# Sums over channels for four kinds of norm: products of split squares with a 0/1 matrix, in place of token-major sums spread back by an identity

## The chip, the cores and the metric

The kernel runs on one core of a Trainium2 chip. The time is that of one execution on the device in microseconds, measured over several runs; a profile is one further execution, read from the hardware profiler's records.

## The reference

The reference is one inference step of a layer with three branches between two half-step SwiGLU FFNs. It takes 512 prompt tokens and 8 x 8 sample tokens, so N = 576 tokens of 1024 channels; all in float32. The places where the change works are the norms, cut out here:

```python
def _rmsnorm(x, g):
    return x * lax.rsqrt(jnp.mean(x * x, axis=-1, keepdims=True) + 1e-6) * g

x = x + 0.5 * _swiglu(_rmsnorm(x, ffn1_norm), ffn1_w_up, ffn1_w_down)
h = _rmsnorm(x, mix_norm)
# RWKV-7 branch: 8 heads of 64 channels
kk = hd(k * k_k)
kk = kk / jnp.maximum(jnp.sqrt(jnp.sum(kk * kk, axis=-1, keepdims=True)), 1e-12)
...  # the recurrence over the tokens gives o
mean = jnp.mean(o, axis=-1, keepdims=True)
var = jnp.mean(jnp.square(o - mean), axis=-1, keepdims=True)
o = (o - mean) * lax.rsqrt(var + 64e-5) * gn_g + gn_b
# convolution branch: 256 channels
cm = jnp.mean(c, axis=-1, keepdims=True)
cv = jnp.mean(jnp.square(c - cm), axis=-1, keepdims=True)
c = (c - cm) * lax.rsqrt(cv + 1e-5) * conv_ln_g + conv_ln_b
...  # cross-attention branch, gated merge
x = x + 0.5 * _swiglu(_rmsnorm(x, ffn2_norm), ffn2_w_up, ffn2_w_down)
y = _rmsnorm(x, final_norm)
```

## The kernel before

**Layout.** Activations are channel-major: 128 channels in the partitions, 576 tokens along the free axis, worked on in two halves of 288. A projection (`mm3k`, L91) is made with float32 accuracy out of three float32r products: weights and activations are each split in two parts (`split`, L76 to L78: a cast by ScalarE to the high part, a subtraction by VectorE to the low part), and high x high, high x low, low x high are added in PSUM. The parts of the weights live in the ring `wq` with three slots each for `wh` and `wl` (`wload`, L64).

**Norms.** A sum over channels runs across partitions. `sums` (L111) takes 128 tokens of the squares as the stationary operand and a column of ones (or two columns, one for each head) as the moving one, in float32: its result is token-major, tokens in the partitions. Square root and reciprocal are then small (3, 5 or 10 columns). `spread` (L122) brings the values back to every channel by a float32 product with the identity, after `heads` (L133) has widened them for the two heads of a tile. Five places use this: the start of both FFNs (`rstd`, `rows`, L263 to L277), the norms that follow the FFNs (half by half, L337 to L370), the convolution's layer norm (L517 to L523), the norm of `kk` in `prep` (L685 to L694), and the group norm in `chain` (L752 to L765).

**Stages.** First comes FFN 1 (until about 425 us), then the three branches, then the merge and FFN 2. The branches follow a list of steps, `PLAN` (L24): P, I, J and B are prep, inverse, joined blocks and chain of one of four pairs of heads; A is the attention, G and C the convolution, X, Y and Z are fillers, projections of the gates and branches (`gate`, `gated`, L625 to L640), nearly all L91. A chain (B) runs eight chunks of 64 tokens one after another (`chunks`, L851): each needs the state of the one before, and goes from products to copies and back four times. Then come the sample chunk, and the group norm.

**Order.** Each engine issues in an order that is fixed when the kernel is built. The framework interleaves the steps of `PLAN` on each engine as far as dependences and buffers let it; a slot of a ring is given in the order of the program, so an instruction that needs a slot stays behind the earlier holders of that slot. TensorE, VectorE and ScalarE then each work through their own list in order; an instruction that waits for another engine holds those behind it.

Of the kernel before, what the change touches and what calls it, by code (L numbers as in the profile page):

```python
# [14 lines left out]
D = 1024  # L15
# [14 lines left out]
# columns of the packed parameter vectors  # L30
# [7 lines left out]
# columns of the packed constants  # L38
# [8 lines left out]
class _Builder:  # L47
# [16 lines left out]
    def wload(self, src, n, pool=None, tag="", cap=512):  # L64
        """A weight tile as two float32r parts whose sum is the float32 weight: f(part, from, to)."""
# [17 lines left out]
    def mm3(self, p, w, x, n, h, m=128):  # L83
        """p = w^T x for half h of the tokens, with float32 accuracy: hi*hi + hi*lo + lo*hi."""
        c = slice(h * H, (h + 1) * H)
        for k in range(n):
            self.mm3k(p, w(0, k * m, (k + 1) * m), w(1, k * m, (k + 1) * m), x[k], c, k, n)
# [5 lines left out]
    def proj(self, src, x, n=8, m=128):  # L93
        """The two halves of w^T x in PSUM."""
        w = self.wload(src, n * m)
        ps = []
        for h in range(2):
            p = self.bank()[:m, :H]
            self.mm3(p, w, x, n, h, m)
            ps.append((slice(h * H, (h + 1) * H), p))  # L100
        return ps

    def full(self, tag, *ops):
        """The two halves of the sum of float32 products lhs [K, 128]^T rhs [K, N] in PSUM."""
# [7 lines left out]
    def sums(self, tag, ops, sel, c):  # L112
        """Sums over channels, as sel [128, w] selects them, for the tokens of c: [128 tokens, block * w] in PSUM."""
# [7 lines left out]

    def spread(self, tag, r, c=slice(0, N)):  # L122
        """Token-major values r [128 tokens, block, 128 channels], 512 tokens at a time, channel-major in PSUM."""
# [9 lines left out]
    def heads(self, t, r):  # L133
        """[128 tokens, (block, head)] as [128 tokens, block, 128 channels], in t"""
        t = t.rearrange("p (b c) -> p b c", c=64)
        self.A.copy(t, r.unsqueeze(2).broadcast_to([128, 10, 64]))
        return t.rearrange("p (b h) c -> p b (h c)", h=2)

    @staticmethod
    def blocks(c):  # L140
        """Blocks of 128 tokens that cover c, as (first token, rows at the start that the block before holds)."""
# [7 lines left out]
    def build(self):  # L149
        tc, a = self.tc, self.a  # L150
        with ExitStack() as st:
# [9 lines left out]
            self.eps = cp.tile([128, 2], F32, name="eps")  # L161
# [9 lines left out]
            with ExitStack() as sf:  # L171
# [16 lines left out]
                self.dma(self.cst, a["cst"])  # L188
                self.G.memset(self.eps[:, 0:1], 64e-5)
                self.G.memset(self.eps[:, 1:2], 1e-5)  # L190
                self.A.activation(self.eps[:, 0:1], self.eps[:, 0:1], AF.Copy)
# [60 lines left out]
    @staticmethod  # L252
    def padded(t):
        """The chunks of 64 + 1 columns and the sample blocks of 8 + 1"""
        return _q8(t[:, :520], 65), _q8(t[:, 520:592], 9)
# [7 lines left out]
    def rstd(self, fp, ss, h):  # L263
        """1/sqrt(mean square + 1e-6) of the tokens of half h, token-major."""
# [6 lines left out]

    def rows(self, fp, t, h):
        """The values t of the tokens of half h in every partition."""
# [13 lines left out]
    def ffn(self, x, hp, fp, g, wu, wd, done, raw=None, mid=None, kv=()):  # L287
        """x += FFN(norm(x)) / 2, the last block of it half by half of the tokens, each handed to done.
        raw: the weights of the first three projections, by 128 input channels, which run as the channels come in."""
# [19 lines left out]
        r = [self.rstd(fp, ss, h) for h in range(2)]  # L309
        r = [self.rows(fp, t, h) for h, t in enumerate(r)]  # L310
# [32 lines left out]
        for i in range(2):  # L343
            s = slice(i * H, (i + 1) * H)
            for m in range(8):
# [4 lines left out]
                if i == 1 and m == 1:  # L350
                    r = self.rstd(fp, ss, 0)
                if i == 1 and m == 3:
                    done(x, fp, slice(0, H), self.rows(fp, r, 0))
# [16 lines left out]
    def mem_k(self):  # L370
        """Memory keys of the prompt, channel-major."""
# [10 lines left out]
    def mem_v(self):  # L382
        """Memory values of the prompt, token-major."""
# [13 lines left out]
    def mem_keep(self, kv):  # L397
        """Keys block-diagonal for a pair of heads, and values."""
# [18 lines left out]
    def shifted(self, m, out, zp):  # L417
        """out = z + (previous z - z) * mu for the m-th 128 channels of the shifted projection."""
# [77 lines left out]
    def conv(self, ap, us):  # L496
# [20 lines left out]
        p = self.sums("g", sq, self.con("ones", 1), slice(0, N))  # L517
        r = ap.tile([128, 5], F32, name="rt")
        A.activation(r, p, AF.Sqrt, scale=1.0 / 256, bias=self.eps[:, 1:2])
        V.reciprocal(r, r)  # L520
        for c, p in self.spread("g", r.unsqueeze(2).broadcast_to([128, 5, 128])):
            for j in range(2):
                V.tensor_tensor(cs[j][:, c], cs[j][:, c], p, ALU.mult)  # L523
# [10 lines left out]
    def softmax(self, ap, p, s):  # L534
        """exp(p / 8 - max) over the last axis of p [128, n, 256] into s; returns the reciprocals of its sums."""
# [11 lines left out]
    def attention(self, ap, op):  # L547
# [8 lines left out]
        # prompt  # L556
# [26 lines left out]
        # samples: the rows of a request are its (head, token) pairs  # L583
# [47 lines left out]
    def gated(self, pool, n, wname, y, i, first):  # L631
        """Adds sigmoid(gate n) * (y @ w) to the merged branches in DRAM (first: writes it)."""
# [10 lines left out]
    def prep(self, j):  # L643
# [6 lines left out]
        def parts(t, o=0):  # L650
            """prompt [128, 8, 64 of q] and sample [128, 8, 8 of q] views of a dense tile"""
# [3 lines left out]
        # decay and its running products within a chunk; a zero column restarts the product  # L655
        sg = b1.tile([128, 640], F32, name="u1", bufs=2)[:, :N]
# [28 lines left out]
        sq = b1.tile([128, 640], F32, name="u1", bufs=2)[:, :N]  # L685
        A.activation(sq, k, AF.Square, scale=par("kk", j))
        p = self.sums("g", [sq], bd[:, ::64], slice(0, N))
        rt = b1.tile([128, 10], F32, name="rt")
        A.activation(rt, p, AF.Sqrt)
        V.tensor_scalar(rt, rt, 1e-12, None, ALU.max)  # L690
        V.reciprocal(rt, rt)
        nr = b1.tile([128, 640], F32, name="u1", bufs=2)[:, :N]
        for c, p in self.spread("g", self.heads(b1.tile([128, 640], F32, name="u1", bufs=2), rt)):
            V.scalar_tensor_tensor(nr[:, c], k[:, c], par("kk", j), p, ALU.mult, ALU.mult)  # L694
# [20 lines left out]
        # products of the rows within a chunk: rows (k, b) by source token, columns (r, a) by token  # L715
# [13 lines left out]
    def chain(self, j):  # L729
# [5 lines left out]
        # token-major keys and values  # L735
# [15 lines left out]
        # group norm, bonus and gate  # L751
        sq, rs = (b3.tile([128, 640], F32, name="u2", bufs=2)[:, :N] for _ in range(2))  # L752
# [6 lines left out]
        p = self.sums("c", [sq], con("bd")[:, ::64], slice(0, N))  # L759
        rt = b3.tile([128, 10], F32, name="rt")  # L760
        A.activation(rt, p, AF.Sqrt, scale=1.0 / 64, bias=self.eps[:, 0:1])
# [309 lines left out]
```

## Time and profile before

| | us |
|---|---|
| median of 3 runs | 1533.83 |
| lowest and highest run | 1531.67, 1535.93 |
| span of the profiled execution | 1531.9 |
| busy: VectorE / ScalarE | 818.2 / 583.4 |
| first sums of FFN 1 / of FFN 1's end | 27.13 / 418.93 |
| recurrence of the last chain, four chunks | 967.1 to 984.2 |

The span of the profiled execution runs from its first to its last instruction. In the rows of the profile, PE is TensorE's products, PEld its loading of stationary operands, DVE is VectorE, ACT is ScalarE; L91 is line 91 of the kernel. A float32 product appears as two records, a float32r product as one.

### The profile page before, as it was taken

Reading aid. Unit: us, or ns where it says so; the run is one execution under the profiler, and the core shown is the slowest. Engines: PE = TensorE matmul, PEld = TensorE weight load, DVE = VectorE, ACT = ScalarE, POOL = GpSimd, SP = SyncE. Lnnn points to the kernel's source line nnn. Section 1 sums busy time; section 2 is a strip of 40 time slices with the busy share of each in tenths; the row PEclk is TensorE's granted clock in tenths of the full one; section 3 lists DMA queues with packets and bytes.
Section 4 is the critical chain, followed back from the end, with each engine's and each line's share of the span. In section 5 each row is a group of like instructions: output and inputs, shape, how many; then the busy total and the mean of one; then the engine's idle time right before and its main releaser. Section 6 shows DMA issues by size and latency. Waiting matters only on the chain.

```text
span 1531.9 us, 26990 instructions
## 1 busy us (share of the span) xinstructions
PE 1505.6 (98%) x11194; PEld 1430.4 (93%) x11194; DVE 818.2 (53%) x1639; ACT 583.4 (38%) x1155; POOL 4.5 (0%) x21
## 2 busy tenths in 40 slices
PE   8999999999999999999999999999999999999997
PEld 8999999999998889878879879889999999999997
DVE  6443344334584559768466455376444434443454
ACT  6232223223457645445346533343332222222331
POOL 0000000000000000000000000000000000000000
PEclk9999999999999999999899999999999999999998
DMA  5222222222533143123223124274212222222231
GB/s 189 83 83 83 84 83 83 83 83 83 163 106 131 38 153 75 58 77 106 63 64 94 52 73 119 67 246 160 84 69 83 83 83 84 83 83 83 84 110 63
DMA packets 90711, 144.64 MB, mean 94 GB/s; under 512 B 43148, under 2 KB 52748, under 8 KB 90588
## 3 DMA queue, kind: packets, MB, share of 16 engines
q1 hardware_dynamic: 90012, 142.33, 28.8%
q8 instruction: 87, 1.43, 0.4%
q10 hardware_dynamic: 576, 0.59, 0.1%
q14 instruction: 36, 0.29, 0.1%
HBM read 126.36 MB, written 16.53 MB: 93 GB/s over the span
## 4 chain that ended last, share of the span: by engine, by line
PE 93%; DVE 3%; ACT 2%; DMA 1%; issue 1%; SPq 0%; DVEq 0%; ACTq 0%
PE p L91 79%; PE g L724 1%; PE c L842 1%; PE c L846 1%; PE c L839 1%; PE g L109 1%; DVE pr L801 1%; PE c L109 1%; PE c L874 1%; PE c L872 1%; DVE tt L803 1%; PE c L857 1%; PE c L894 0%; PE p L129 0%; PE g L129 0%
## 5 line engine op out<-in xcount | busy, mean ns | idle before, releaser
L91 PE MATMUL p<-xh,wl 128*128 128x288 f32 (+1 forms) x2080 | 620.9, 299 | 1.5 <-DVE wl L78 1.5
L91 PE MATMUL p<-xl,wh 128*128 128x288 f32 (+1 forms) x2080 | 621.9, 299 | 0.0
L91 PE MATMUL p<-xh,wh 128*128 128x288 f32 (+1 forms) x2080 | 620.9, 299 | 0.9 <-ACT r L276 0.6
L77 ACT CAST wh<-w 128x512 fp32r<-128x512 f32 (+1 forms) x371 | 226.1, 611 | 558.0 <-PE p L91 540.2
L91 PEld LDWEIGHTS p<-xh,wh 128*128 128x128 f32 (+1 forms) x2080 | 391.6, 188 | 8.0 <-issue 3.1
L91 PEld LDWEIGHTS p<-xh,wl 128*128 128x128 f32 (+1 forms) x2080 | 391.4, 188 | 7.2 <-issue 3.3
L91 PEld LDWEIGHTS p<-xl,wh 128*128 128x128 f32 (+1 forms) x2080 | 391.7, 188 | 6.5 <-issue 4.4
L78 DVE TENSOR_TENSOR wl<-w,wh 128x512 fp32r<-128x512 f32 (+1 forms) x371 | 251.5, 679 | 265.4 <-ACT wh L77 252.7
L91 PE MATMUL p<-hl,wh 128*128 128x288 f32 x512 | 151.0, 295 | 0.0
L91 PE MATMUL p<-hh,wh 128*128 128x288 f32 x512 | 151.0, 295 | 0.0
L91 PE MATMUL p<-hh,wl 128*128 128x288 f32 x512 | 150.7, 294 | 0.0
L91 PEld LDWEIGHTS p<-hh,wl 128*128 128x128 f32 x512 | 96.1, 188 | 0.0
L91 PEld LDWEIGHTS p<-hl,wh 128*128 128x128 f32 x512 | 96.1, 188 | 0.0
L91 PEld LDWEIGHTS p<-hh,wh 128*128 128x128 f32 x512 | 96.0, 188 | 0.0
L326 DVE TENSOR_TENSOR t<-p,r 128x288 f32<-128x288 f32 x88 | 40.2, 457 | 90.6 <-PE p L91 90.6
L337 DVE SCALAR_TENSOR_TENSOR x<-p,x 128x288 f32<-128x288 f32 x64 | 29.3, 458 | 68.9 <-PE p L91 68.9
L77 ACT CAST hh<-t 128x576 fp32r<-128x576 f32 (+1 forms) x50 | 30.8, 616 | 77.5 <-DVE t L331 57.5
L91 PE MATMUL p<-hh,whd 128*128 128x288 f32 x192 | 56.9, 296 | 0.0
L91 PE MATMUL p<-hl,whd 128*128 128x288 f32 x192 | 56.5, 294 | 0.0
L91 PE MATMUL p<-hh,wld 128*128 128x288 f32 x192 | 56.5, 294 | 0.0
L320 DVE TENSOR_TENSOR t<-p,r 128x288 f32<-128x288 f32 x88 | 39.9, 455 | 24.4 <-PE p L91 21.3
L78 DVE TENSOR_TENSOR hl<-t,hh 128x576 fp32r<-128x576 f32 (+1 forms) x50 | 34.3, 686 | 33.2 <-ACT hh L77 33.2
(312 smaller groups left out, 1887.0 us busy)
## 6 DMA issues: line engine op xcount, KB each, us to landing
w<-wu SPq DMA_DIRECT2D x85, 512.0 KB
w<-win SPq DMA_DIRECT2D x44, 512.0 KB
w<-wd SPq DMA_DIRECT2D x32, 512.0 KB
w<-wd SPq DMA_DIRECT2D x16, 384.0 KB
d_mb<-gate SPq DMA_DIRECT2D x16, 288.0 KB
w<-wo SPq DMA_DIRECT2D x8, 512.0 KB
x<-x SPq DMA_DIRECT2D x8, 288.0 KB
d_x<-x SPq DMA_DIRECT2D x16, 144.0 KB
```

The lines of the kernel that those rows point to most:

```text
L77: self.A.copy(hi, x)
L78: self.V.tensor_tensor(lo, x, hi.bitcast(F32), ALU.subtract)
L91: self.T.matmul(p, l, x[r][:, c], start=k == 0 and i == 0, stop=k == n - 1 and i == 2)
L109: self.T.matmul(p, l, r[:, c], start=i == 0, stop=i == len(ops) - 1)
L320: V.tensor_tensor(t1[:, c], q, ri, ALU.mult)
L326: V.tensor_tensor(t2[:, c], q, ri, ALU.mult)
L337: V.scalar_tensor_tensor(x[m][:, c], p, 0.5, x[m][:, c], ALU.mult, ALU.add)
L724: T.matmul(ps[:, i * 128:(i + 1) * 128], kb[o, c + i].rearrange("p a t -> p (a t)"), ra[o, c + i].rearrange("p a t -> p (a t)"), start=Tru ...
L801: V.tensor_tensor(pr, tt[:, :n, :e].unsqueeze(2).broadcast_to([np_, n, m, e]), l3[:, t:e, :e].unsqueeze(1).broadcast_to([np_, n, m, e]), A ...
L803: V.tensor_reduce(tt[:, :n, t:e], pr, op=ALU.add, axis=AX.X)
L839: T.matmul(ps[64:, 64 * h:64 * h + 64], gr[:64, h, c, 64:], vu[:64, c, 64 * h:64 * h + 64], start=h == 0 or not inter, stop=not inter)
L842: T.matmul(ps[64:, :128], l, r, start=False, stop=i == len(inter) - 1)
```

## The change

`sums` stays for one use; `heads` is gone. The new `totals` splits the squares as weights and activations are split, into slots of the same ring `wq`, and multiplies both parts by a 128 x 128 matrix of zeros and ones as the stationary operand, 288 tokens at a time. The products are float32r, and their result is channel-major already: each channel holds the sum of its group. Square root and reciprocal then run over 288 or 576 columns in 128 partitions instead of 3, 5 or 10 columns. At the end of an FFN only the first half of the tokens goes this way; the second half keeps `rstd` and `rows`. Two copies of the 0/1 matrices are cast once at the start. The lines of the changed kernel lie some 12 further on (L869 is L857 of before, L884 L872, L886 L874, L854 L842, L851 L839, L858 L846, L769 L756), and comments were taken out.

```diff
+    def totals(self, tag, t, sel, c=slice(0, N)):
+        for o in range(c.start, c.stop, H):
+            hl = [self.wq.tile([128, 512], F32R, name="w" + i)[:, :H] for i in "hl"]
+            self.split(hl[0], hl[1], t[:, o:o + H])
+            p = self.bank(tag)[:, :H]
+            for i, t_ in enumerate(hl):
+                self.T.matmul(p, sel, t_, start=i == 0, stop=i == 1)
+            yield slice(o, o + H), p
...
+            self.sel = {t: cp.tile([128, 128], F32R, name="sel" + t) for t in ("ones", "bd")}
...
+    def rfull(self, fp, ss, h):
+        r = fp.tile([128, H], F32, name="r" + str(h), bufs=1)
+        for _, p in self.totals("p", ss, self.sel["ones"], slice(h * H, (h + 1) * H)):
+            self.A.activation(r, p, AF.Sqrt, scale=1.0 / D, bias=self.eps[:, 2:3])
+        self.V.reciprocal(r, r)
+        return r
...
-        r = [self.rstd(fp, ss, h) for h in range(2)]
-        r = [self.rows(fp, t, h) for h, t in enumerate(r)]
+        r = [self.rfull(fp, ss, h) for h in range(2)]
...
                 if i == 1 and m == 1:
-                    r = self.rstd(fp, ss, 0)
+                    r = self.rfull(fp, ss, 0)
                 if i == 1 and m == 3:
-                    done(x, fp, slice(0, H), self.rows(fp, r, 0))
+                    done(x, fp, slice(0, H), r)
...
-        p = self.sums("g", sq, self.con("ones", 1), slice(0, N))
-        r = ap.tile([128, 5], F32, name="rt")
-        A.activation(r, p, AF.Sqrt, scale=1.0 / 256, bias=self.eps[:, 1:2])
+        V.tensor_tensor(sq[1], sq[0], sq[1], ALU.add)
+        r = ap.tile([128, N], F32, name="sg", bufs=2)
+        for c, p in self.totals("g", sq[1], self.sel["ones"]):
+            A.activation(r[:, c], p, AF.Sqrt, scale=1.0 / 256, bias=self.eps[:, 1:2])
         V.reciprocal(r, r)
-        for c, p in self.spread("g", r.unsqueeze(2).broadcast_to([128, 5, 128])):
-            for j in range(2):
-                V.tensor_tensor(cs[j][:, c], cs[j][:, c], p, ALU.mult)
+        for j in range(2):
+            V.tensor_tensor(cs[j], cs[j], r, ALU.mult)
...
-        p = self.sums("g", [sq], bd[:, ::64], slice(0, N))
-        rt = b1.tile([128, 10], F32, name="rt")
-        A.activation(rt, p, AF.Sqrt)
-        V.tensor_scalar(rt, rt, 1e-12, None, ALU.max)
-        V.reciprocal(rt, rt)
-        nr = b1.tile([128, 640], F32, name="u1", bufs=2)[:, :N]
-        for c, p in self.spread("g", self.heads(b1.tile([128, 640], F32, name="u1", bufs=2), rt)):
-            V.scalar_tensor_tensor(nr[:, c], k[:, c], par("kk", j), p, ALU.mult, ALU.mult)
+        nr = b1.tile([128, N], F32, name="u1", bufs=2)
+        for c, p in self.totals("g", sq, self.sel["bd"]):
+            A.activation(nr[:, c], p, AF.Sqrt)
+        V.tensor_scalar(nr, nr, 1e-12, None, ALU.max)
+        V.reciprocal(nr, nr)
+        V.scalar_tensor_tensor(nr, k, par("kk", j), nr, ALU.mult, ALU.mult)
...
-        p = self.sums("c", [sq], con("bd")[:, ::64], slice(0, N))
-        rt = b3.tile([128, 10], F32, name="rt")
-        A.activation(rt, p, AF.Sqrt, scale=1.0 / 64, bias=self.eps[:, 0:1])
+        rt = b3.tile([128, N], F32, name="u2", bufs=2)
+        for c, p in self.totals("c", sq, self.sel["bd"]):
+            A.activation(rt[:, c], p, AF.Sqrt, scale=1.0 / 64, bias=self.eps[:, 0:1])
         V.reciprocal(rt, rt)
-        for c, p in self.spread("c", self.heads(b3.tile([128, 640], F32, name="u2", bufs=2), rt)):
-            V.tensor_tensor(rs[:, c], rs[:, c], p, ALU.mult)
+        V.tensor_tensor(rs, rs, rt, ALU.mult)
```

The change also moves instructions that it does not name. The first place is TensorE in one chunk of the last chain. This is the list of before, from the product with the state that gives the outputs (c<-ra,st) to the one that gives the next state (c<-vu,kbt); the rows p<- are projections of a filler, with xh and xl the two parts of the activations.

```order
L874 MATMUL c<-ra,st_4891 128x64
L842 MATMUL c<-st_4892,ra 64x128
L91 MATMUL p<-xh_4502,wl 128x288
L91 MATMUL p<-xh_4488,wh 128x288
L91 MATMUL p<-xl_4489,wh 128x288
L839 MATMUL c<-vu,gr 64x64 x2
L91 MATMUL p<-xh_4488,wl 128x288
L846 MATMUL c<-xs,gr 64x64 x2
L91 MATMUL p<-xh_4490,wh 128x288
L91 MATMUL p<-xl_4491,wh 128x288
L91 MATMUL p<-xh_4490,wl 128x288
L857 MATMUL c<-vu,kbt 128x128
```

This is the same piece of the list of the changed kernel:

```order
L886 MATMUL c<-ra,st_4885 128x64
L854 MATMUL c<-st_4883,ra 64x128
L851 MATMUL c<-vu,gr 64x64 x2
L858 MATMUL c<-xs,gr 64x64 x2
L869 MATMUL c<-vu,kbt 128x128
L884 MATMUL c<-gr,vu 64x64 x2
```

The projections are gone from between the chunk's products; in the four chains, 30 chunk updates stand like this, and only two intervals between updates (one each in the second and third chain) hold projections, 96 and 66 of them, in a row.

The second place is TensorE at the group norm of the first chain, before: c<-ra,cst are the products that subtract the mean, c<-cst,u the sums.

```order
L756 MATMUL c<-ra,cst 128x320
L756 MATMUL c<-ra,cst 128x256
L91 MATMUL p<-xl_4493,wh 128x288
L91 MATMUL p<-xh_4492,wl 128x288
L91 MATMUL p<-xh_4494,wh 128x288
L91 MATMUL p<-xl_4495,wh 128x288
L91 MATMUL p<-xh_4494,wl 128x288
L119 MATMUL c<-cst,u_7041 128x2 x2
L91 MATMUL p<-xh_4496,wh 128x288
L91 MATMUL p<-xl_4497,wh 128x288
```

And after, with c<-wh,selbd and c<-wl,selbd the new products of the split squares, and c<-lg,wg those of the branch's output gate:

```order
L769 MATMUL c<-ra,cst 128x320
L769 MATMUL c<-ra,cst 128x256
L129 MATMUL c<-wh,selbd 128x288 x2
L109 MATMUL c<-lg_4879,wg_4870 128x288
L129 MATMUL c<-wl,selbd 128x288
L109 MATMUL c<-aux,wg_4871 128x288
L129 MATMUL c<-wl,selbd 128x288
L91 MATMUL p<-xh_4481,wh 128x288
L91 MATMUL p<-xl_4482,wh 128x288
```

The five projections between the centering and the first sums are gone; the new products follow the centering at once, and the projections come behind them.

More of the change, by code (lines that the diff above doesn't have):

```diff
@@ L131, in spread @@
             yield d, p
[L133 to L137, printed above, removed]
     @staticmethod
@@ L160, in build @@
             self.cst = cp.tile([128, _NCC], F32, name="cst")
-            self.eps = cp.tile([128, 2], F32, name="eps")
+            self.eps = cp.tile([128, 3], F32, name="eps")
+            self.sel = {t: cp.tile([128, 128], F32R, name="sel" + t) for t in ("ones", "bd")}
             self.omu = cp.tile([128, 15], F32, name="omu")
@@ L188, in build @@
                 self.dma(self.cst, a["cst"])
+                for t, s in self.sel.items():
+                    self.A.copy(s, self.con(t))
                 self.G.memset(self.eps[:, 0:1], 64e-5)
                 self.G.memset(self.eps[:, 1:2], 1e-5)
+                self.G.memset(self.eps[:, 2:3], 1e-6)
                 self.A.activation(self.eps[:, 0:1], self.eps[:, 0:1], AF.Copy)
@@ L654, in prep @@
         k, r, v = tmp("k"), tmp("r"), b2.tile([128, N], F32, name="v")
-        sg = b1.tile([128, 640], F32, name="u1", bufs=2)[:, :N]
+        sg = b1.tile([128, N], F32, name="u1", bufs=2)
         for c, p in self.full("g", (self.wda[:64, 128 * j:128 * j + 128], self.la[:64])):
@@ L684, in prep @@
         self.shifted(4 + j, k, b1)
-        sq = b1.tile([128, 640], F32, name="u1", bufs=2)[:, :N]
+        sq = b1.tile([128, N], F32, name="u1", bufs=2)
         A.activation(sq, k, AF.Square, scale=par("kk", j))
-        p = self.sums("g", [sq], bd[:, ::64], slice(0, N))
-        rt = b1.tile([128, 10], F32, name="rt")
-        A.activation(rt, p, AF.Sqrt)
-        V.tensor_scalar(rt, rt, 1e-12, None, ALU.max)
-        V.reciprocal(rt, rt)
-        nr = b1.tile([128, 640], F32, name="u1", bufs=2)[:, :N]
-        for c, p in self.spread("g", self.heads(b1.tile([128, 640], F32, name="u1", bufs=2), rt)):
-            V.scalar_tensor_tensor(nr[:, c], k[:, c], par("kk", j), p, ALU.mult, ALU.mult)
+        nr = b1.tile([128, N], F32, name="u1", bufs=2)
[4 more added lines that the diff above has]
+        V.scalar_tensor_tensor(nr, k, par("kk", j), nr, ALU.mult, ALU.mult)
         for o, x, y in zip(ra_a, parts(nr), before):
@@ L749, in chain @@
         self.sample_chunk(j, gr, kbt, vu, ra, gc)
-        sq, rs = (b3.tile([128, 640], F32, name="u2", bufs=2)[:, :N] for _ in range(2))
+        sq, rs = (b3.tile([128, N], F32, name="u2", bufs=2) for _ in range(2))
         for c0, c1 in ((0, 5), (5, 9)):
@@ L899, in sample_chunk @@
             s = slice(64 * h, 64 * h + 64)
-            vx = b3.tile([128, 640], F32, name="u2", bufs=2)[:, :NB * 64].rearrange("p (b v) -> p b v", v=64)
+            vx = b3.tile([128, N], F32, name="u2", bufs=2)[:, :NB * 64].rearrange("p (b v) -> p b v", v=64)
             V.tensor_tensor(vx, vu[:, 8:9, s].broadcast_to([128, NB, 64]),
```

## The prediction

> **What bounds the kernel now.** The first views are the page's busy times, the shares of the chain of waits, and the clock row of the slices.
>
> ```profile
> span 1531.9 us, 26990 instructions
> PE 1505.6 (98%) x11194; PEld 1430.4 (93%) x11194; DVE 818.2 (53%) x1639; ACT 583.4 (38%) x1155; POOL 4.5 (0%) x21
> PE 93%; DVE 3%; ACT 2%; DMA 1%; issue 1%; SPq 0%; DVEq 0%; ACTq 0%
> PEclk9999999999999999999899999999999999999998
> ```
>
> TensorE is busy for 98% of the span, 93% of the chain that ended last is its work, and it runs almost always at full clock. So two things move the time: work that leaves TensorE, and any place where it has to wait that it did not have before. The second view cuts the span into stretches. After the span come busy time and count of PE, PEld, DVE, ACT and POOL, then the granted clock, the DMA share and GB/s.
>
> ```profile
> 30.00:420.00 390.00, 390.00 (x2932) 389.81 (x2933) 177.94 (x310) 113.18 (x182) 0.00 (x0) 1.00 0.27 89
> ...
> 737.30:740.70 3.40, 3.40 (x74) 3.15 (x73) 1.65 (x6) 0.83 (x3) 0.00 (x0) 1.00 0.17 55
> 740.70:744.10 3.40, 3.40 (x21) 3.34 (x19) 1.01 (x2) 0.58 (x1) 0.00 (x0) 0.51 0.02 5
> ...
> 945.60:949.00 3.40, 1.36 (x36) 1.25 (x37) 0.00 (x0) 1.31 (x5) 0.00 (x0) 0.99 0.94 279
> 949.00:952.40 3.40, 3.40 (x41) 3.19 (x39) 0.42 (x1) 1.43 (x4) 0.00 (x0) 0.50 0.20 66
> ```
>
> The first row is the first FFN: 390.00/2932 = 0.133 us for each product of 128x288 (nearly all are L91's). The others show what happens where L91 is missing. A stretch of 3.4 us whose 74 products are small ones is followed by one at clock 0.51, though PE counts as busy throughout. A stretch with PE busy for only 1.36 us is followed by 0.50. The third view is L91 alone in two stretches (busy PE, busy PEld, clock).
>
> ```profile
> 737.30:740.70 3.40, 0.00 (x0) 0.00 (x0) 1.00 0.17 55
> ...
> 967.10:984.20 17.10, 10.85 (x53) 7.52 (x53) 1.00 0.22 74
> ```
>
> The first of them had no L91. The second is four chunks of the last chain, with 53 L91, 13 for each chunk, and a clock of 1.00. **The chains are covered by the fillers' projections now.** The last view is the timeline of one chunk there:
>
> ```profile
> 977.51 0.34 PE L872 MATMUL c<-gr,vu 128*64 128x64 f32 x4
> 977.78 0.43 PE L874 MATMUL c<-ra,st 128*128 128x64 f32 x2
> 978.14 0.43 PE L842 MATMUL c<-st,ra 128*64 128x128 f32 x2
> 978.67 0.26 ACT L844 COPY xs<-c 64x128 f32<-64x128 f32 x1 [0.20 <-PE c L842]
> ...
> 979.80 0.44 PE L846 MATMUL c<-xs,gr 64*64 64x64 f32 x4
> 980.28 0.26 ACT L848 COPY vu<-c 64x128 f32<-64x128 f32 x1 [1.35 <-PE c L846]
> 980.67 0.41 PE L857 MATMUL c<-vu,kbt 128*128 128x128 f32 x2
> 981.12 0.58 DVE L866 SCALAR_TENSOR_TENSOR st<-c,gc,mg 64x64 f32<-64x64 f32 x2 [2.21 <-PE c L857]
> 981.80 0.34 PE L872 MATMUL c<-gr,vu 128*64 128x64 f32 x4
> ```
>
> From L872 to the next L872 a chunk takes 981.80 - 977.51 = 4.29 us, of which 13 x 0.133 = 1.73 is work for the fillers. The chunk itself costs PE 2.56.
>
> **The change part by part. 1, PE work removed.** These rows are the sums (L119) and the spreading (L129) of one prep, of the convolution, and of the first FFN.
>
> ```profile
> 607.80 1.28 PE g L119 x10
> 613.57 1.41 PE g L129 x10
> ...
> 809.23 1.90 PE g L119 x18
> 814.26 2.07 PE g L129 x10
> ...
> 27.13 1.39 PE L119 MATMUL p<-cst,ss 128*128 128x1 f32 x12
> 28.95 2.02 PE L129 MATMUL p<-cst,rt 128*128 128x128 f32 x12 [0.43 <-DVE rt L269]
> 30.90 0.61 PE L91 MATMUL p<-xh,wh 128*128 128x288 f32 x1
> ...
> 418.93 0.72 PE L119 MATMUL p<-cst,ss 128*128 128x1 f32 x6
> 424.39 0.94 PE L129 MATMUL p<-cst,rt 128*128 128x128 f32 x6
> ```
>
> A prep or chain loses 1.28 + 1.41 less 0.16, since a group's modelled end laps over the next start: 2.53. It gains four products like L91's, 4 x 0.133 = 0.53. Eight places at -2.0 make **-16**. The convolution loses 1.90 + 2.07 - 0.16 and gains 0.53: **-3.3**. At the start of an FFN, PE now needs 30.90 - 27.13 = 3.77 from the first sum to the next projection. After, it waits for a cast and a subtraction (0.43 and 0.45, rows below), two products, a table load and a square root of half width (1.28 and an estimated 0.45), together about 2.7: -1.1, twice, **-2.2**. The half-width reciprocal there is hidden by two banks of projections (2 x 24 x 0.133 = 6.4 us). An FFN's end saves 0.72 + 0.94 - 0.27 = 1.4, twice: **-2.8**. Together **-24.3**.
>
> **2, the naked recurrence.** The new split tiles stand in the weights' ring ahead of the fillers' weights, and the fillers' products stay behind them. By the order rows above, L91 no longer stands between a chunk's products. This is so for 30 chunk updates in the four chains (8, 7, 7, 8); only two chunk intervals, in the second and third chain, have L91 in them (96 and 66 rows). A naked chunk takes its chain of dependences, from the rows above: DVE 0.58, +0.10 to L872, 0.27 to L874, 0.36 to L842, its 0.43, +0.10, copy 0.26, L846 0.44, +0.04, copy 0.26, L857 0.41, +0.04; that is 3.29, and with an estimated 0.07 ahead of L846 and of L857, 3.43. Against 2.56 this is +0.87 a chunk, 30 x 0.87 = +26, at full clock. At half clock each product takes longer:
>
> ```profile
> L742 PE MATMUL c<-cst,kb 128*128 128x128 f32 x9 | 1.6, 272 | 0.0
> L742 PE MATMUL c<-cst,kb 128*128 128x128 f32 x4 | 1.1, 434 | 0.0
> ```
>
> The same float32 product lasts 272 ns at full clock (from 600 to 640 us) and 434 ns in the half-clock stretch from 740.8 us. Five dependent stages of PE (L872, L874, L842, L846, L857) grow by 0.16 to 0.27 each (the pitch of 0.27 doubled is the upper end), so by 0.8 to 1.35; I take 1.0, a chunk of 4.4, +1.84: 30 x 1.84 = **+55**, with ends of 26 and 66. I take half clock, because a chunk alone is 18 small products in over 3.4 us, nearer to the 36 of the row at 945.60, which was followed by 0.50, than to the row at 967.10.
>
> **3, the rest of the naked stretches.** The sample chunk, the centering products and L109 add some 200 rows of order in the four chains, two records each. At half clock a record costs 0.16 more where PE is the limit: 400 x 0.16 = 64 at most, 0 if all of it hides in waits. Most are short (8 columns), and every second one waits for a copy anyway: **+15**.
>
> **4, centering to totals.** The timeline of the first chain's norm, and the groups of the split's two steps:
>
> ```profile
> 673.04 0.43 ACT L757 COPY u<-c 128x320 f32<-128x320 f32 x1 [3.49 <-PE c L756]
> ...
> 673.50 0.47 ACT L758 ACTIVATE u<-u 128x320 f32<-128x320 f32 x1
> 673.88 0.35 ACT L757 COPY u<-c 128x256 f32<-128x256 f32 x1
> ...
> L77 ACT CAST xh<-t 128x288 fp32r<-128x288 f32 x16 | 6.9, 434 | 7.4 <-DVE t L413 7.4
> L78 DVE TENSOR_TENSOR xl<-t,xh 128x288 fp32r<-128x288 f32 x16 | 6.9, 453 | 0.0
> ...
> L761 ACT ACT_TABLE_LOAD x4 | 5.1, 1283 | 0.1
> L666 DVE RECIPROCAL w<-g 128x592 f32<-128x592 f32 x4 | 15.4, 3855 | 0.1
> ```
>
> Now five projections stand between centering and sums. After, nothing does: copy 0.43, square 0.47, copy 0.35, square about 0.42, cast 0.43 twice and subtraction 0.45 make 2.98 until the last product, less 0.53 in which PE works on the others: 2.4 x 4 = **+10** (0 to 14). Queued behind these products on PE are L109 and all the fillers' L91. The reciprocal of 128x576 (3.76 us, the L666 row times 576/592, in place of one of 10 columns) is hidden there: the fillers held back now follow.
>
> **5, preps and convolution.** The totals wait for the same split, with few projections ahead in places, and hold ring slots that casts of weights wait for. Bounds are 0 and 5 x 3.6 = 18 (both halves' split, 1.76, and as much again for the ring); nearest is the 2.4 above with some cover: **+10**.
>
> **6, the clock at the seams.** A half-clock window costs 1.7 us of PE work. Some three of before's lie where the new ones would swallow them (-5), and L91 resumes cold in four places (+5): **0**.
>
> Sum: -24.3 + 55 + 15 + 10 + 10 = +65.7; 1531.9 + 65.7 = 1597.6. The median of the runs, 1533.83, stands 1.9 above the span of the profiled execution, so the forecast is **1599 us**.
>
> **The rivals. Full clock.** If the clock stays at 1.00 in the naked recurrence, terms 2 and 3 are 26 and 0, and term 6 is -5: -24.3 + 26 + 10 + 10 - 5 = +17, **1550 us**. For it: naked chunks still have PE at work for half of the time (18 products in 3.43 us). Against it: the row at 737.30, with no idle time and 74 products, did not keep the clock.
>
> The Trainium skill says, on the page "TensorE: Matmul & The Clock Gate" in Part 1, that half rate comes back after an idle window of about 3.4 us, and full rate after a busy one. By that rule a recurrence that works in every window would keep full clock and this rival would hold. The row at 740.70 of this trace (0.51 behind a window busy for 3.40 of 3.40) speaks against such a reading, so it gets a minor chance.
>
> **Reciprocals in the recurrence.** The change has nine more reciprocals of 128x576. Where DVE, which works in order, has one ahead of L866's update, the whole chain stands still, and no filler covers it now: 9 x 3.76 = 34 at most, +65.7 + 34 = +100, **1634 us**. Against it: four belong to the norms behind the recurrences, and not every prep lies beside a chain.
>
> **Not slower: PE work decides.** If a naked chunk's dependences fitted beside the sample chunk's and the next products, waits would cost nothing and only term 1 stays: 1531.9 - 24.3 + 1.9 = **1510 us**. It decides as soon as the 30 chunks lose less than 24.3/30 = 0.81 each and terms 3 to 5 vanish. The 98% of busy PE speaks for it; the 3.43 of dependences, 0.87 over the work, against.
>
> **No gain at all.** If products with the 0/1 matrix cost what float32 products do (two passes, about 0.27 each, so 40 x 0.4 = +16 over term 1's price) while the fillers cover the waits, the two sides nearly cancel: about **1526 to 1538 us**.
>
> **How the numbers follow.** Forecast 0.58 (1575 to 1625), full clock 0.20 (1540 to 1575), reciprocals or everything at its upper end 0.12, only PE work 0.06, no gain 0.04. The range of 1545 to 1635 takes in the forecast, most of the full-clock case and half of the heavy one. A measurement of this kernel can tell about 0.3% from no change, which is 4.6 us. Faster by more 0.06, within it 0.04, slower by more 0.90.
>
> **What would show it.** In the windows over a chain's recurrence: no L91, PE busy for about half, a clock of 0.50, and 4.4 us from one c<-gr,vu product with four records to the next (3.4 if the clock stays at 1.00, 4.3 with L91 between if the order has no effect). In the timeline behind the centering: PE idle for about 2.4 us until the first products with selbd. In the groups: 40 products at about 0.13 us of pitch, and no L119 but the FFNs' second halves. In DVE's rows: a reciprocal of 3.8 us just ahead of an update of st would show the heavy rival. The prediction is wrong if the chunks' period stays at 4.3 with L91 in it, or if the clock is 1.00 where L91 is missing.

## The result and the profile after

The changed kernel takes 1642.16 us (median of 4 runs, 1641.13 to 1649.98) against 1534.88 us for the kernel before, measured beside it: a ratio of 1.0708, 95% interval 1.0672 to 1.0743. It is slower, as forecast, but by 107 us where 65 had been forecast, and the time lies 7 us above the range.

The page of the changed kernel, in the rows that were shown of before (span, busy times, shares of the chain by engine, granted clock in 40 slices):

```profile
span 1639.3 us, 26653 instructions
PE 1539.7 (94%) x10980; PEld 1451.4 (89%) x10980; DVE 870.0 (53%) x1648; ACT 593.4 (36%) x1178; POOL 4.6 (0%) x22
...
PEclk9999999999997999688869969779999999999999
...
PE 84%; DVE 8%; ACT 5%; issue 2%; DMA 1%; SPq 0%; DVEq 0%; ACTq 0%
```

TensorE falls from 98% to 94% of a longer span, work of VectorE and ScalarE makes up 13% of the chain that ended last (5% before), and the clock has holes between the 13th and the 27th slice, which is where the attention and the chains lie. The stretches of the changed kernel (busy PE, PEld, DVE, ACT, POOL, then the clock): two chunks of the last chain, one chunk of the third, and the first part of the attention.

```profile
1048.82:1053.47 4.65, 3.61 (x19) 2.56 (x19) 0.57 (x2) 1.14 (x4) 0.00 (x0) 0.50 0.00 0
1053.47:1058.12 4.65, 3.61 (x19) 2.56 (x19) 0.57 (x2) 1.13 (x4) 0.00 (x0) 0.50 0.01 4
968.14:971.58 3.44, 1.99 (x15) 1.29 (x15) 0.57 (x2) 1.43 (x6) 0.00 (x0) 1.00 0.00 0
483.00:550.10 67.10, 56.56 (x305) 43.97 (x303) 32.70 (x66) 48.36 (x117) 0.00 (x0) 0.87 0.10 32
```

L91 alone in three chunks:

```profile
1048.82:1062.76 13.94, 0.00 (x0) 0.00 (x0) 0.50 0.00 1
```

A chunk without projections takes 4.65 us at a clock of 0.50; the one at a clock of 1.00 takes 3.44. For the attention, the same part of it in the kernel before is this row:

```profile
481.10:540.30 59.20, 58.61 (x382) 47.98 (x380) 32.45 (x72) 42.19 (x112) 0.00 (x0) 1.00 0.13 44
```

TensorE was busy for 58.61 of 59.20 us there, at full clock; after, it is busy for 56.56 of 67.10 us at a clock of 0.87. The timeline of one of the chunks at a clock of 0.50, in the places of the chunk shown of before:

```profile
1053.47 0.80 PE L869 MATMUL c<-vu,kbt 128*128 128x128 f32 x2 [0.35 <-ACT vu L860]
1054.30 0.60 DVE L878 SCALAR_TENSOR_TENSOR st<-c,gc,mg 64x64 f32<-64x64 f32 x2 [4.05 <-PE c L869]
...
1054.96 0.48 PE L884 MATMUL c<-gr,vu 128*64 128x64 f32 x4 [0.69 <-DVE st L878]
1055.37 0.69 PE L886 MATMUL c<-ra,st 128*128 128x64 f32 x2
1055.98 0.69 PE L854 MATMUL c<-st,ra 128*64 128x128 f32 x2
...
1056.77 0.26 ACT L856 COPY xs<-c 64x128 f32<-64x128 f32 x1 [0.46 <-PE c L854]
1057.08 0.69 PE L858 MATMUL c<-xs,gr 64*64 64x64 f32 x4
1057.80 0.26 ACT L860 COPY vu<-c 64x128 f32<-64x128 f32 x1 [0.78 <-PE c L858]
1058.12 0.58 PE L869 MATMUL c<-vu,kbt 128*128 128x128 f32 x1 [0.35 <-ACT vu L860]
```

The chain of dependences is the one that the prediction added up, with PE's stages at half speed and PE idle in between ([0.69 <-DVE st], [0.35 <-ACT vu]).

**Where the time went.** The traces are compared by stretches: each stretch's length, less 0.133 us for every L91 product in it, is what it costs beyond its projections; both traces have 9360 L91 products in all. The forecast's terms are sorted into the same stretches.

| stretch | before | after | change | forecast |
|---|---|---|---|---|
| first chunk to centering, four chains | 96.3 | 177.8 | +81.5 | +70 (terms 2, 3) |
| attention and prep 0 | 50.1 | 68.9 | +18.8 | 0 |
| FFN 1, and all behind the last centering | 42.6 | 43.9 | +1.3 | -4.6 |
| the rest between the chains | 98.0 | 103.8 | +5.8 | +0.3 |
| sum | 287.1 | 394.4 | +107.4 | +65.7 |

A chain's row runs from its first product c<-vu,kbt to its centering; the attention's runs from its first product to the first product of the joined blocks. Of the 41.7 us that the forecast lacked, 18.8 stand in the attention with prep 0, 11.5 in the recurrences, 5.9 in the row of the FFNs and 5.5 between the chains.

### The profile page after: what moved, and what is told of

It reads as the page before. It is cut to its first block, busy times and chain, and to the rows that moved or that the text cites. A ratio compares the mean times of both kernels' runs of the same rounds, so it can differ in the third digit from the quotient of the medians.

```text
span 1639.3 us, 26653 instructions
## 1 busy us (share of the span) xinstructions
PE 1539.7 (94%) x10980; PEld 1451.4 (89%) x10980; DVE 870.0 (53%) x1648; ACT 593.4 (36%) x1178; POOL 4.6 (0%) x22
## 4 chain that ended last, share of the span: by engine, by line
PE 84%; DVE 8%; ACT 5%; issue 2%; DMA 1%; SPq 0%; DVEq 0%; ACTq 0%
PE p L91 70%; PE c L854 2%; DVE pr L813 2%; PE c L869 1%; DVE tt L815 1%; PE c L109 1%; PE c L886 1%; DVE wl L78 1%; PE g L737 1%; PE c L858 1%; PE c L851 1%; PE c L906 1%; DVE cc L522 1%; PE c L884 1%; DVE st L878 1%
## 5 line engine op out<-in xcount | busy, mean ns | idle before, releaser
L91 PE MATMUL p<-xh,wh 128*128 128x288 f32 (+1 forms) x2080 | 625.3, 301 | 10.3 <-ACT r L284 4.0
L91 PE MATMUL p<-xh,wl 128*128 128x288 f32 (+1 forms) x2080 | 621.5, 300 | 9.0 <-DVE wl L78 9.0
L91 PE MATMUL p<-xl,wh 128*128 128x288 f32 (+1 forms) x2080 | 623.5, 300 | 0.0
L77 ACT CAST wh<-w 128x512 fp32r<-128x512 f32 (+1 forms) x371 | 225.3, 611 | 570.4 <-PE p L91 545.2
L91 PEld LDWEIGHTS p<-xh,wh 128*128 128x128 f32 (+1 forms) x2080 | 398.7, 192 | 18.5 <-ACT r L284 4.5
L91 PEld LDWEIGHTS p<-xh,wl 128*128 128x128 f32 (+1 forms) x2080 | 396.5, 191 | 13.5 <-DVE wl L78 12.1
L91 PEld LDWEIGHTS p<-xl,wh 128*128 128x128 f32 (+1 forms) x2080 | 398.1, 191 | 2.9 <-issue 2.5
L91 PE MATMUL p<-hl,wh 128*128 128x288 f32 x512 | 151.2, 295 | 0.0
L91 PE MATMUL p<-hh,wh 128*128 128x288 f32 x512 | 151.2, 295 | 0.0
L91 PE MATMUL p<-hh,wl 128*128 128x288 f32 x512 | 150.9, 295 | 0.0
L91 PEld LDWEIGHTS p<-hh,wl 128*128 128x128 f32 x512 | 96.3, 188 | 0.0
L91 PEld LDWEIGHTS p<-hh,wh 128*128 128x128 f32 x512 | 96.1, 188 | 0.0
L91 PEld LDWEIGHTS p<-hl,wh 128*128 128x128 f32 x512 | 96.1, 188 | 0.0
L352 DVE SCALAR_TENSOR_TENSOR x<-p,x 128x288 f32<-128x288 f32 x64 | 29.3, 458 | 68.9 <-PE p L91 68.9
L91 PE MATMUL p<-hl,whd 128*128 128x288 f32 x192 | 56.6, 295 | 0.0
L91 PE MATMUL p<-hh,wld 128*128 128x288 f32 x192 | 56.6, 295 | 0.0
L91 PE MATMUL p<-hh,whd 128*128 128x288 f32 x192 | 56.6, 295 | 0.0
L878 DVE SCALAR_TENSOR_TENSOR st<-c,gc,mg 64x64 f32<-64x64 f32 x56 | 15.9, 283 | 75.9 <-PE c L869 75.0
L77 ACT CAST hh<-t 128x576 fp32r<-128x576 f32 (+1 forms) x50 | 30.7, 616 | 69.1 <-DVE t L346 49.7
L335 DVE TENSOR_TENSOR t<-p,r 128x288 f32<-128x288 f32 x88 | 39.5, 453 | 23.6 <-PE p L91 23.5
```

Source lines behind the costliest of these rows:

```text
L77: self.A.copy(hi, x)
L91: self.T.matmul(p, l, x[r][:, c], start=k == 0 and i == 0, stop=k == n - 1 and i == 2)
L335: V.tensor_tensor(t1[:, c], q, ri, ALU.mult)
L352: V.scalar_tensor_tensor(x[m][:, c], p, 0.5, x[m][:, c], ALU.mult, ALU.add)
L878: V.scalar_tensor_tensor(mn[s, s], ps[s, 256 + 64 * h:320 + 64 * h], gc[s, c:c + 1], mg[s, s], ALU.mult, ALU.add)
```

## The experiments

**The theory** was that of the prediction: the split tiles take slots of the weights' ring ahead of the fillers' weights, so the fillers cannot come between a chunk's products (called the ring below). **The rival**: the norms' own work does it, by waits for the split, full-width roots and reciprocals on engines that work in order. Where a run's number of projections between two state products is given, it is counted in that run's trace.

**1. No split.** The products take the squares as they are.

```diff
-            hl = [self.wq.tile([128, 512], F32R, name="w" + i)[:, :H] for i in "hl"]
-            self.split(hl[0], hl[1], t[:, o:o + H])
             p = self.bank(tag)[:, :H]
-            for i, t_ in enumerate(hl):
-                self.T.matmul(p, sel, t_, start=i == 0, stop=i == 1)
+            self.T.matmul(p, sel, t[:, o:o + H], start=True, stop=True)
...
```

> The changed kernel with one thing else: the sums over channels are float32 products of the squares as they are with the float32 0/1 matrix, so there is no split and no tile of the weights' ring; square roots and reciprocals stay full width. If the ring is the cause (the split tiles stand in it ahead of the fillers' weights and hold the fillers back), the fillers come back into the recurrences: about 13 projections in a chunk's interval, a period near 4.3 us, clock 1.00 there, and with term 1 of the prediction less some 5 us for the dearer products about 1515 to 1530 us. If the norms' own work is the cause (full-width square roots and reciprocals, waits of TensorE for statistics), most of it is still there: over 1600 us.

Measured: 1552.6 us, ratio 1.0121 (1.0079 to 1.0163). The recurrences cost 108.8 beyond their projections (96.3 before, 177.8 after), with 6 to 29 projections in a chunk's interval. So 90 of the 107 us went with the split. It missed the expected 1515 to 1530 all the same: something else costs about 19 us over before, and the attention with prep 0 still costs 58.8 in place of 50.1.

**2. The chains' norm as before, the rest changed.**

```diff
-        for c, p in self.totals("c", sq, self.sel["bd"]):
+        p = self.sums("c", [sq], con("bd")[:, ::64], slice(0, N))
...
+        for c, p in self.spread("c", self.heads(b3.tile([128, 640], F32, name="u2", bufs=2), rt)):
...
```

> The changed kernel with the chains' group norm as before; FFNs, convolution and preps changed. If the ring is the cause, the recurrences and sample chunks get their fillers back: by the traces they cost 177.9 us beyond their projections after and 96.3 before, so 1642 - 82 + 8 (the chains' dearer sums) = about 1570 us. If the norms' own work is the cause, only the four chain norms go: 1642 - 15 = about 1627 us.

Measured: 1565.18 us, 1.0213 (1.0185 to 1.0241), near the ring's 1570. The recurrences cost 109.7.

**3. The chains' norm alone changed.** The diff is that of the change, in `chain` only.

> The kernel of before with the chains' group norm alone changed (and comments and tile widths as after). If the ring is the cause: 1534 + 82 - 8 = about 1608 us, with no projection in any chunk's interval. If the norms' own work is the cause: 1534 + 4 x 2.4 = about 1545 us.

Measured: 1627.1 us, 1.0616 (1.0586 to 1.0646): more than the ring's 1608, far from the rival's 1545. No chunk's interval has a projection, and the recurrences cost 189.5.

**4. The ring alone.** The kernel of before gets two pairs of tiles that nothing reads:

```diff
+        for o in (0, H):
+            hl = [self.wq.tile([128, 512], F32R, name="w" + i)[:, :H] for i in "hl"]
+            self.split(hl[0], hl[1], sq[:, o:o + H])
         p = self.sums("c", [sq], con("bd")[:, ::64], slice(0, N))
```

> The kernel of before, in which each chain also splits its squares into two pairs of tiles of the weights' ring that nothing reads; the sums stay as before, and no product is added or taken away. If the ring is the cause: naked recurrences, 1534 + 82 = about 1615 us. If the norms' own work is the cause: eight casts and subtractions off the critical path, within 5 us of 1534.

Measured: 1636.15 us, 1.0678 (1.066 to 1.0696). Not one product is added, taken away or made dearer, the norm is that of before, and the kernel loses 103 us. One chunk of its last chain:

```profile
1045.00:1049.65 4.65, 3.61 (x18) 2.56 (x18) 0.57 (x3) 1.13 (x4) 0.00 (x0) 0.50 0.00 0
```

The row is that of the changed kernel: 4.65 us, PE 3.61, clock 0.50. The time is 21 us over the expected 1615. The run has the split's casts and subtractions in it besides the tiles; run 12, which keeps the split and leaves the ring, tells the two apart. Together they decide for the ring.

**5. Is it TensorE's idle share that halves the clock?** Eleven small products per chunk are added; the diff shows five of them.

```diff
             T.matmul(ps[:, 256:384], kbt[:, c, :], vu[:, c, :], start=True, stop=True)
+            for _ in range(5):
+                T.matmul(ps[:, 448:512], self.dum, self.dum[:, :64], start=True, stop=True)
...
```

> The changed kernel with work added: in every chunk (and the sample chunk) of the chains eleven float32 products of 128x128 by 128x64, written to unused columns of the chunk's PSUM bank and read by nobody, 3 behind the state's product, 3 behind the second solve product, 5 behind the next state's product. The order of everything else stays. If TensorE's idle share is what halves the clock in the naked recurrences, the clock there goes to 1.00, a chunk's period falls from 4.65 to 3.5 to 3.8 us, and the time falls by some 20 us in spite of the added work, to about 1615 to 1625. If the clock doesn't depend on it, the products lengthen the gaps that they stand in, and the time rises to 1650 or more.

Measured: 1776.72 us, 1.1592 (1.1563 to 1.162). One chunk in the windows, and two rows of its neighbour's timeline (L864 is the added product, L865 the copy behind the second solve product):

```profile
1163.95:1173.63 9.68, 8.58 (x41) 7.41 (x41) 0.57 (x2) 1.14 (x4) 0.00 (x0) 0.50 0.00 0
```

```profile
1181.42 1.54 PE L864 MATMUL c<-cst 128*128 128x64 f32 x6
1182.99 0.26 ACT L865 COPY vu<-c 64x128 f32<-64x128 f32 x1 [2.24 <-PE c L864]
```

PE is now busy for 8.58 of 9.68 us, 89%, and the clock is still 0.50. The added products write to unused columns of the chunk's own PSUM tile, and the copy starts only when they are done ([2.24 <-PE c L864]), so they stand on the path (a chunk takes 9.67 us). So the time tells nothing of the clock's worth; the row tells that a busy share of 89%, in small products, did not raise it.

**6. The same with long products in a bank of their own.** There are four in a chunk; the diff shows the two behind the next state's product.

```diff
+        self.pd, self.dm = self.bank("g")[:, :H], bv
...
             T.matmul(ps[:, 256:384], kbt[:, c, :], vu[:, c, :], start=True, stop=True)
+            for _ in range(2):
+                T.matmul(self.pd, vu[:, c, :], self.dm[:, :H], start=True, stop=True)
...
```

> The changed kernel with work added once more, now in a PSUM bank of its own, so that no copy has to wait for it: in every chunk of the chains four float32 products with 288 columns, read by nobody, one behind the state's product, one behind the second solve product, two behind the next state's product; each takes as operand what the recurrence has just made, so that they stand in those places in TensorE's order. If long products keep the clock up, as the fillers' do: clock 1.00 in the naked recurrences, each added product about 0.53 us, a period of about 4.0 us in place of 4.65, and a time of 1615 to 1630 us, less than without them. If the clock stays at 0.50: 1.06 us each, a period of 6 to 7 us, over 1690 us.

Measured: 1644.13 us, 1.0717 (1.069 to 1.0743).

```profile
1060.00:1064.49 4.49, 4.49 (x27) 2.79 (x27) 0.57 (x2) 1.13 (x4) 0.00 (x0) 1.00 0.00 0
1064.49:1068.98 4.49, 4.49 (x28) 2.79 (x27) 0.57 (x2) 1.14 (x4) 0.00 (x0) 1.00 0.01 4
```

With four long products more, the chunk is shorter than without them (4.49 in place of 4.65), and the clock is 1.00 throughout 21 of the 28 chunk intervals (6 in the changed kernel). But the same products do not always bring the clock to 1.00. In the first chain TensorE waits 2.47 us for a state update, and in the chunks behind that wait the clock is 0.50. The rows are the end of the wait, and a later chunk with the same products:

```profile
672.05 0.48 PE L892 MATMUL c<-gr,vu 128*64 128x64 f32 x4 [2.47 <-DVE st L886]
...
684.25:692.72 8.47, 8.47 (x31) 5.11 (x30) 3.04 (x8) 1.14 (x4) 0.00 (x0) 0.50 0.00 0
```

That chunk takes 8.47 us, and TensorE is busy throughout it. The time as a whole did not fall: the recurrences cost 205.1 us beyond their projections (177.8 in the changed kernel), and the stretches between the chains 20 less. In the plain chunks at a clock of 1.00 the first expectation nearly holds, with 4.12 to 4.49 us in place of 4.0; neither expectation has the time.

**7. The FFNs' norms alone, without a split.**

```diff
+            self.T.matmul(p, sel, t[:, o:o + H], start=True, stop=True)
...
+        for _, p in self.totals("p", ss, self.con("ones"), slice(h * H, (h + 1) * H)):
...
-        r = [self.rstd(fp, ss, h) for h in range(2)]
-        r = [self.rows(fp, t, h) for h, t in enumerate(r)]
+        r = [self.rfull(fp, ss, h) for h in range(2)]
...
```

> The kernel of before with only the FFNs' norms changed, with float32 products in place of the split (no ring). By term 1 of the prediction, less some 1 us for the dearer products: 1534 - 4 = about 1530 us. If full-width reciprocals at the FFN's start hold TensorE, no change or some us slower.

Measured: 1522.96 us, 0.9926 (0.9905 to 0.9947): faster than both kernels, by more than expected.

**8. The FFNs' norms alone, with the change's split.**

> The kernel of before with only the FFNs' norms changed, now as the change has them (split in the weights' ring; the 0/1 matrix is cast at each FFN's start). By term 1: 1534 - 5 = 1529 us. By the stretch of the first FFN in the changed kernel's trace (16.9 us beyond its projections, 15.0 before, 10.6 with float32 products), the split gives the gain back: 1532 to 1536 us.

Measured: 1531.74 us, 0.9978 (0.9964 to 0.9992). So the split gives most of the gain back, as the second figure had it. The start of FFN 1, first in the changed kernel, then in run 7:

```profile
30.30 0.40 PE L91 MATMUL p<-xh,wh 128*128 128x288 f32 x1 [2.12 <-ACT r L284]
...
40.52 0.40 PE L91 MATMUL p<-xh,wh 128*128 128x288 f32 x1 [1.53 <-ACT wh L77]
```

```profile
29.31 0.40 PE L91 MATMUL p<-xh,wh 128*128 128x288 f32 x1 [1.44 <-ACT r L283]
```

After the first wait (for the root) the changed kernel waits once more ten us later, for the cast of the next weights, which stands late in ScalarE's list; run 7 starts 1 us earlier and has no second wait of 0.4 us or more there. In the stretches that hold the FFNs, run 8 costs 13.9 and 25.8 us beyond the projections, run 7 10.8 and 23.6.

**9. The preps' norm alone changed**, split and all.

> The kernel of before with only the preps' norm changed, as in the changed kernel (split in the weights' ring). If prep 0's tiles in the ring uncover the attention, the stretch of the attention costs about 69 us beyond its projections (50 before), and the total is 1534 + 19 + 13 (recurrences as in the run with the old chains) - 6 = about 1560 us. If only the full-width reciprocal that stands between two softmax steps counts there, as in the float32 run, the attention costs about 59 and the total is near 1543.

Measured: 1572.89 us, 1.0257 (1.0239 to 1.0274). The attention with prep 0 costs 69.9 beyond its projections, the recurrences 110.6. So the attention's loss is there whole without any change in the chains, and 14 of the recurrences' 81.5 us. The time is 13 us over the expected 1560: the stretches between the chains cost 6.6 more than before, where a gain of 6 had been expected.

**10. No split, preps as before.** FFNs, convolution and chains as in run 1.

> The changed kernel with float32 products of the unsplit squares (no ring) in FFNs, convolution and chains, and the preps' norm as before. If the preps' full-width reciprocals and the order around them are what is left of the loss in the all-float32 run (1553 us), about 1522 to 1532 us, faster than before. If the rest lies in the chains' norms, about 1540 or more.

Measured: 1533.63 us, 0.9999 (0.9986 to 1.0013), 1.6 us over the expected range. The preps make out 19 us of run 1, so they are its remaining loss over before. Next to run 7, the chains and the convolution changed without a ring lose 11 us, so of the norms changed here only the FFNs' gain.

**11. FFNs and convolution without a split.**

> The run with the FFNs' norms alone in float32 products (1523 us) with the convolution's layer norm added, also as float32 products without a split; preps and chains as before. By term 1 another 3 us less, about 1520 us, the fastest version here. If the convolution's full-width square root, reciprocal and order cost as much as they save: 1523 to 1528 us.

Measured: 1524.83 us, 0.9952 (0.992 to 0.9984). The convolution's part can't be told from nothing next to run 7's 1522.96.

**12. The chains with their split in tiles of their own** (64 columns each).

```diff
+                for q in range(0, H, 64):
+                    e = min(q + 64, H)
+                    hl = [self.sq.tile([128, 64], F32R, name="s" + i)[:, :e - q] for i in "hl"]
+                    self.split(hl[0], hl[1], t[:, o + q:o + e])
...
```

> FFNs' norms in float32 products (alone 1523 us), preps and convolution as before, and the chains' group norm as in the changed kernel, split and all, but with the two parts in small tiles of their own (64 columns, ten pairs of products for a chain's 576 tokens) instead of the weights' ring. If it is the ring and not the split, the fillers stay between the chunks' products and the time is 1523 to 1540 us. If the split itself (its waits, the full-width root and reciprocal) is what uncovers the recurrence, about 1600 us, near the run with the chains alone changed (1627 us).

Measured: 1548.84 us, 1.0096 (1.0079 to 1.0112), 9 us over the expected range and 78 below run 3; 11 of the 78 are the FFNs' gain of run 7, which run 3 does not have. All chunk intervals have 11 to 18 projections (29 in the very first), and the recurrences cost 99.4. So the split doesn't uncover the recurrence when its tiles are not in the weights' ring. The medians of this run and run 7 differ by 26 us, the two traces by 19. Most of that lies behind the norms: behind the third and the last centering the stretches cost 19.0 and 29.6, against 10.8 and 23.6, with one wait of 6.5 us between the last chain's norm and the merge.

## Why the prediction was right and where it was wrong

**The direction and the mechanism held.** Runs 3, 4 and 12 show the ring as the cause of the naked recurrences: the tiles alone uncover them, and the split without the ring does not.

**Term 2, the naked recurrence: right in kind, low in size, and the clock was 0.50 only in part.** Of the 26 chunk intervals without a projection, 8 had a clock of 0.50 throughout, 5 had 1.00, and 13 had both. The price of a plain chunk was near: at full clock 3.44 in the chunk shown (estimated 3.43; the other four intervals take 2.93 to 4.07), at half clock 4.65 against 4.4 taken, a growth of 1.21 inside the bounds of 0.8 to 1.35. So a plain chunk at half clock costs 2.09 more than before, against 1.84, and one at full clock less than that. All 28 chunk intervals cost 144.8 beyond their projections against 74.8 before: 70.0 more, where term 2 said 55, and 66 as its upper end. What it left out are the intervals with other work in them. In each chain the sixth holds products of the sample chunk and takes 7.25 to 7.47 us (12.0 more than before, in all four; term 3 had meant these products). Two hold products of the next pair's prep, which stood outside the chunk intervals before (9.84 and 7.31 us, 12.0 more together), and one a long reciprocal (4.9 more, shown below). From the last update to the centering the chains cost 33.0 against 21.5. Terms 2 and 3 together are +81.5 in place of +70.

**The step that failed is term 5**, which put preps and convolution at +10 with 18 as its upper end; for prep 0 that left nothing, +2 for its wait against the 2 that it saves by term 1. It looked for naked places in the chains alone, and took prep 0's norm as one wait for a split. But prep 0 stands beside the attention, whose products wait for softmax in the same way as a chunk's for its copies. The attention with prep 0 cost 18.8 us more, which is more than term 5's upper end for all preps and the convolution together. Two things add up there. One is the full-width reciprocal of the rival, which I had priced in the recurrence; it sits in the attention (these are rows of the changed kernel's timeline: L706 is the new reciprocal, L555 and L558 softmax, L581 the next product):

```profile
519.10 3.75 DVE L706 RECIPROCAL u<-u 128x576 f32<-128x576 f32 x1
...
522.91 0.68 DVE L555 TENSOR_REDUCE mx<-c 128x2 f32<-128x512 f32 x1
...
525.00 0.47 ACT L558 ACTIVATE s<-c,mx 128x256 f32<-128x256 f32 x1
...
525.62 0.89 PE L581 MATMUL c<-cst,s 128*128 128x128 f32 x4 [2.50 <-ACT s L558]
```

The maximum of the next softmax step stands behind 3.75 us of reciprocal, and TensorE waits 2.50 us. The reciprocal is not alone in that wait: behind the maximum come 0.81 us of another step of the prep on VectorE (L707) and a table load of 1.28 us on ScalarE, which ends at 524.99, just ahead of the exponential.

The other thing is the ring. These rows lie ahead of prep 0's new sums (the L129 row, the first of them):

```profile
499.17 1.03 PE L591 MATMUL c<-vm,pt 128*128 128x64 f32 x4 [2.03 <-ACT pt L584]
...
505.72 1.14 PE L581 MATMUL c<-cst,s 128*128 128x128 f32 x4 [2.23 <-ACT s L558]
...
510.97 0.59 PE L129 MATMUL g<-wh,selbd 128*128 128x288 f32 x1
```

From 496 us to these sums there is no projection, and TensorE waits for softmax; run 9 has the same two waits, 2.03 and 2.23 us. Run 1 has neither: at the same place of its attention, the 10 us from 493.7, it has 45 projections, and its waits of 2.51 and 2.03 us stand behind its reciprocal. Without the ring (run 1) the attention costs 8.7 us more than before; with it (run 9, after) 19 to 20. So the rest, 10 to 11 us, goes with the split and its tiles in the ring; the tiles alone, as in run 4, were not tried here. Nor are the 8.7 of run 1 the reciprocal's alone: run 10, with the preps' norm of before, costs 53.3 there, 3.2 more than before. How the remaining 5.5 divide between the reciprocal, the table load and the half clock behind the waits was not tried.

**Term 1: too high a gain in the FFNs.** It gave -5 for them with the split; the trace shows +1.3 in the stretches that hold them, and alone they gain 3 (run 8). The working had 2.7 us from the first sum's split to the next projection at the start (its five parts, 0.43, 0.45, two products of 0.13, 1.28 and 0.45, add up to 2.9). TensorE resumed 30.30 - 27.48 = 2.8 us after the first new product, with the split itself beside projections; what the working left out is the second wait, of 1.53 us, at 40.52. Without the split the gain is there, 11 us in run 7.

**Terms 4 and 6** cannot be told apart in the stretches between the chains, which cost 5.8 more with 0.3 forecast. In the first chain, PE's group of centering products starts at 696.85 and the first new product at 699.93, held by the cast ([0.79 <-ACT wh L77]):

```profile
696.85 2.29 PE L769 MATMUL c<-ra,cst 128*128 128x320 f32 x4
...
699.44 0.43 ACT L77 CAST wh<-u 128x288 fp32r<-128x288 f32 x1
...
699.93 0.61 PE L129 MATMUL c<-wh,selbd 128*128 128x288 f32 x1 [0.79 <-ACT wh L77]
```

The idle time there is shorter than the 2.4 us taken. The centering takes 2.29 us (1.48 before), and the first copy and most of the first square run beside it.

**The rivals.** Full clock (1550) is refuted by the time and by the 0.50, though 5 of the 26 intervals without projections had it. The Trainium skill's rule on the page "TensorE: Matmul & The Clock Gate", Part 1, that half rate comes back after an idle window, would have kept the clock at 1.00 in windows where PE works for 3.61 of 4.65 us; this trace has 0.50 there, and run 5 has it at 8.58 of 9.68. The measurement decides. The heavy rival (1634) came nearest in time, but by luck: its mechanism shows in the recurrences only once inside a naked chunk, and with a reciprocal that the kernel had before:

```profile
664.84 3.85 DVE L681 RECIPROCAL w<-g 128x592 f32<-128x592 f32 x1
...
669.34 0.48 PE L884 MATMUL c<-gr,vu 128*64 128x64 f32 x4 [3.53 <-DVE st L878]
```

That chunk takes 7.49 us in place of 4.65. None of the nine new reciprocals stands in a naked chunk.

## What to carry to other kernels

A short-lived tile taken from a ring that feeds an unrelated stream orders that stream behind it: look at the order of the engine's list on both sides before counting instructions, and look at every stage that lives on filler work, not only the longest one. Price a covered stage by its own chain of dependences at the clock that it would have alone, and price apart the places in it that hold other work. Be wary of widening statistics that are tiny when token-major on an engine that stands between two dependent steps; here only the FFNs' norms gained from it, 3 us with the split (run 8) and 11 without (run 7).

## What the runs showed of the hardware

In these traces the clock does not follow TensorE's busy time. It stayed at 0.50 with PE busy for 78% (after) and 89% (run 5) of a chunk, in products of 64 to 128 columns. It was 1.00 in most chunks with four float32 products of 288 columns more (run 6, PE busy throughout, 27 records in 4.49 us), but 0.50 in chunks with the same products in the first chain, where PE was busy throughout too (8.47 of 8.47 us). So neither the busy share nor the products of the chunk alone decide; no run here separates the length of the products, the share of columns streamed and what went before, and the condition itself stays open. And a copy out of PSUM waited 2.24 us for products that wrote other columns of the same tile (run 5); whether the chip or the framework's own ordering asks for that wait, no run tells.
